# Building the state-space output matrices on one engine, and working more expert blocks ahead of the gates

## The chip, the cores and the metric

The kernel runs on one core of a Trainium2 chip. The metric is the device time of one execution in microseconds (us), the median of several. The engines are TensorE (PE; its weight loads are shown as PEld), VectorE (DVE), ScalarE (ACT), GpSimd (POOL) and SyncE (SP), which only issues DMAs here.

## What is computed

Two layers over 512 latent tokens and 256 context tokens of width 1024. Layer 0 mixes tokens with a bidirectional diagonal state-space model, layer 1 with latent attention. After each mixer comes an expert channel mixer: each token chooses 128 of 16384 experts, and

```
out = sum over k of gelu(h . U[idx_k]) * gate_k * V[idx_k]
```

In layer 0 the state-space part is, for 64 groups of 16 channels and 64 complex states each, in both directions,

```
h[t] = A h[t-1] + B u[t]          (A diagonal, complex)
y[t] = Re(C h[t]), both directions summed, plus d * u[t]
o    = (gelu(y) * sigmoid(gelu(y) @ w_glu)) @ w_o
```

The context is scanned first and hands its last state to the latent tokens. A modulation (scale, shift and gate per channel, from `ada_w`) is computed from the conditioning vectors.

## The kernel before

**Writing order.** Each stage is a Python generator that yields a planned cost after each piece of work. `merge` advances the stream whose clock is lowest, which sets the order in which instructions are written down; the streams after `side=` are advanced the same way but need not end. The framework then orders each engine's instructions by that order and by when it believes operands are ready, and waits for a free buffer where a pool has none. `t4` tiles (4 KB per partition, 20 buffers), `t2` tiles (2 KB, 8 buffers) and `row` tiles (5 buffers) are shared by all stages.

**State-space layer.** The 768 tokens are 96 chunks of eight. `s5_prep` brings the inputs to chunk states `X`; `s5_scan` runs 47 steps of four small VectorE instructions each (L645 twice, L656, L657), each planned at `TS` = 0.95; `s5_fill` completes the states in between for one block of four group pairs (VectorE L495, L498, then ScalarE L669 to L671, which reorder real and imaginary parts). `s5_mout` builds the output matrices: 8 blocks times 2 directions, each piece two halves of three elementwise instructions (L626, L627, L628) into a `t4` tile `Mout` and a `t2` scratch `tqm`, planned at `TM`. Before, a piece runs on GpSimd unless its number `b * 2 + d` is in `MV`, where it runs on VectorE. `s5_readout` goes over eight blocks: TensorE multiplies the inputs with a Toeplitz kernel `Tt` (L694) and the states with `Mout` (L697), ScalarE applies GELU (L700), TensorE turns the result (L714) and VectorE copies it out of PSUM to `yc` and `yl` (L716, L717). `products` asks `mout` for matrices as it needs them. The scan is merged with `mout` and with the modulation stream `rest` (96 tiles `ada_wt` in all, TensorE L197) beside it, the readout with `rest`. Then follow the GLU (`zp`, L762) and the output projection.

**Expert mixer.** Four tiles of 128 tokens in layer 0 and three in layer 1 are computed densely: every expert's activation, times a gate matrix that is mostly zero. The other tiles (two, then one) gather rows of U and V by index (L1287 on GpSimd's queue), with one VectorE instruction for each row (L1294, L1299); the gather's rows are spread over the other work by planned cost. For the dense tiles:

- A *U block* (128 experts) is split into a high and a low fp32r part (ScalarE L305, then VectorE or GpSimd L306), multiplied in 24 matmuls `s_ps` (L1149), and passed through GELU (L1152).
- *Gates*: one-hot matrices on VectorE (L1080, L1088), widened on ScalarE (L1085), multiplied into `g_ps` (L1102), copied to `stage` (L1104) and stored to DRAM as `gm`.
- *V blocks*: the gated activations times V in `acc` (L1219, the last half in L1240).

`ahead` works the first `A0` (layer 0) or `A1` (layer 1) U blocks before or while the gates are made, with the low part on GpSimd, and stores the activations to DRAM (`ged`). `dense` reloads them; for the other blocks the low part is VectorE's. A reloaded block is charged `-XM` = -2.0 in the plan, a fresh one 5.2 (times three quarters in layer 1). `peer` merges the gates with all but the last `TL` = 3 of the blocks worked ahead and has the gather beside them, then merges `dense` with the gather:

```
merge(self.gates, most(), side=(self.gathering,))
merge(self.dense(l), self.gathering)
```

Dense works in groups of eight blocks, first V on half the columns, then on the other half; where the next group's blocks are all worked ahead, their gating is mixed into the second half.

Of the kernel before, what the change touches and what calls it, by code (L numbers as in the profile page):

```python
# [15 lines left out]
ALU = mybir.AluOpType  # L16
# [5 lines left out]
KD = 8  # L22
# [3 lines left out]
NCH = 96  # L26
CH_CTX = 32
# [14 lines left out]
NPOOL = 0  # L42
FA = 1.0
R0, R1 = 2.25, 3.0
A0, A1 = 40, 48
GA = 5
TL, PW, XM = 3, 2, 2.0
FG0, FG1 = 50.0, 5.0
KB = 2
TP, TM, TS, TA = 4.7, 6.5, 0.95, 1.6  # L50
LA, LD = 2, 5
LT = 3
PA, FP = 20, 3.0
# [1 line left out]
AT = 2  # L55
E0, E1, E2 = 0, 11, 5
YB, YC = 1, 17
NF, MV = 2, (11, 13, 15)


def dap(t, off, ap):
    return bass.AP(tensor=t.tensor, offset=t.offset + off, ap=ap)
# [45 lines left out]
class Net:  # L108
# [240 lines left out]
    def s5_params(self):  # L349
# [106 lines left out]
        for r, op in ((0, ALU.subtract), (1, ALU.add)):  # L456
            w3 = self.t4([128, 64, 16], "w3")
            E = (V, GP)[r]
            E.tensor_tensor(out=fB[r], in0=Bt[r], in1=frb, op=ALU.mult)
            E.tensor_tensor(out=w3, in0=Bt[1 - r], in1=fib, op=ALU.mult)  # L460
            E.tensor_tensor(out=fB[r], in0=fB[r], in1=w3, op=op)
        self.ada0 = ada

    def s5_input(self):
# [10 lines left out]
        for s in (1, 0):  # L475
            c0, n = ((CH_CTX, 64), (0, CH_CTX))[s]
            for x in range(2):
                us = self.u[x][:, :, c0:c0 + n]
                m = [ms[s][:, i, x * 4:(x + 1) * 4, :].rearrange("p k r -> p (k r)").unsqueeze(2).to_broadcast([128, 32, n])
                     for i in range(2)]  # L480
                E = (V, GP)[x]
                E.tensor_tensor(out=us, in0=us, in1=m[1], op=ALU.mult)
                E.tensor_tensor(out=us, in0=us, in1=m[0], op=ALU.add)
# [116 lines left out]
    def s5_mout(self):  # L600


        GP, V = self.nc.gpsimd, self.nc.vector
        NB, pq = 4, self.pq
        sh = [128, 4, 8, 16]
        self.Mout = {}
        C = {}
        for d in range(2):
            for i in range(2):
                C[d, i] = self.t4([128, 32, 2, 16], f"cc{i}")  # L610
                self.load(C[d, i], self.a["s5_cc"][:, i, d * 32:(d + 1) * 32])
            self.nc.scalar.mul(C[d, 0][64:128], C[d, 0][64:128], -1.0)
        for b in range(8):
            for d in range(2):
                M = self.Mout[d, b] = self.t4([128, NB, 2, 128], "Mout")
                for h in range(2):
                    g0 = b * NB + h * 2
                    mo = M[:, h * 2:h * 2 + 2].rearrange("p g x (j c) -> p (g x) j c", j=8)
                    if d:
                        mo = mo[:, :, ::-1, :]  # L620
                    p = [pq[r][:, :, d * 32 + g0:d * 32 + g0 + 2, :].rearrange("p k g x -> p (g x) k").unsqueeze(3)
                         .to_broadcast(sh) for r in range(2)]
                    c = [C[d, i][:, g0:g0 + 2].rearrange("p g x c -> p (g x) c").unsqueeze(2).to_broadcast(sh) for i in range(2)]
                    tq = self.t2(sh, "tqm")
                    E = V if b * 2 + d in MV else GP
                    E.tensor_tensor(out=mo, in0=p[0], in1=c[0], op=ALU.mult)  # L626
                    E.tensor_tensor(out=tq, in0=p[1], in1=c[1], op=ALU.mult)  # L627
                    E.tensor_tensor(out=mo, in0=mo, in1=tq, op=ALU.subtract)  # L628
                yield TM

    def s5_scan(self):
# [41 lines left out]
    def s5_readout(self, mout):  # L673

        nc = self.nc
        V, S, PE = nc.vector, nc.scalar, nc.tensor
        X = self.X
        self.yT = {1: [], 0: []}

        def kernels(fb):  # L680
            Tt = self.t4([128, 8, 128], "Tt")
            for j in range(8):
                self.load(Tt[j * 16:(j + 1) * 16], dap(self.kext, fb * 8 * 3840 + (7 - j) * 16, [[240, 16], [3840, 8], [1, 128]]))
            return Tt

        def products(fb, Tt):
            while (1, fb) not in self.Mout:
                next(mout)
            yp = [self.ps([NCH, 4, 128], f"yp{g2}") for g2 in range(2)]
            for gi in range(8):  # L690
                g = fb * 8 + gi
                gp, g2 = g // 2, g % 2
                o = yp[g2][:, gi // 2, :]
                PE.matmul(out=o, lhsT=self.u[g // 32][:, g % 32, :], rhs=Tt[:, gi, :], start=True, stop=False)  # L694
                for d in range(2):
                    dg = d * 32 + gp
                    PE.matmul(out=o, lhsT=X[:, :, g2, dg], rhs=self.Mout[d, fb][:, gp % 4, g2, :], start=False, stop=(d == 1))  # L697
            Y = self.t4([NCH, 8, 8, 16], "Y")
            for g2 in range(2):
                S.activation(out=Y[:, :, g2::2, :].rearrange("p j g c -> p g j c"),  # L700
                             in_=yp[g2].rearrange("p g (j c) -> p g j c", j=8), func=AF.Gelu)
            return Y

        def turn(fb, Y):
            if fb % 4 == 0:
                self.yT[1].append(self.t4([128, 4, T_CTX], "yc"))
            if fb % 2 == 0:
                self.yT[0].append(self.t4([128, 2, T_LAT], "yl"))
            yc = self.yT[1][-1][:, fb % 4, :].rearrange("p (c j) -> p j c", j=8)
            yl = self.yT[0][-1][:, fb % 2, :].rearrange("p (c j) -> p j c", j=8)  # L710
            for j4 in range(2):
                tp = self.ps([128, 4, NCH], "ytp")
                for j in range(4):
                    PE.transpose(out=tp[:, j, :], in_=Y[:, j4 * 4 + j].rearrange("p g c -> p (g c)"),  # L714
                                 identity=self.ident[0:NCH, 0:NCH])
                V.tensor_copy(out=yc[:, j4 * 4:j4 * 4 + 4, :], in_=tp[:, :, 0:CH_CTX])  # L716
                V.tensor_copy(out=yl[:, j4 * 4:j4 * 4 + 4, :], in_=tp[:, :, CH_CTX:NCH])  # L717

        Y = None
        Tt = kernels(0)  # L720
        yield 0.0
        for fb in range(NF):
            self.s5_fill(fb)
        for fb in range(KD):
            if fb + NF < KD:
                self.s5_fill(fb + NF)
            nxt = kernels(fb + 1) if fb + 1 < KD else None
            last, Y = Y, products(fb, Tt)
            Tt = nxt
            if last is not None:  # L730
                turn(fb - 1, last)
            yield 8.0
        turn(KD - 1, Y)

    def load_w(self, src, name, n=D):
# [899 lines left out]
```

## Time and profile before

| | |
|---|---|
| median of 3 runs | 4044.7 us (4038.66 to 4044.82) |
| profiled execution, its own time | 4041.79 us |
| span of its profile | 4040.0 us |
| mean granted TensorE clock | 0.955 |
| PE busy | 3658.0 us (91%) |
| DVE busy | 3263.9 us (81%) |
| POOL busy | 1650.8 us (41%) |
| ACT busy | 1494.6 us (37%) |

Busy is the time in which an engine had an instruction in work, waiting inside it included. Line numbers are those of the kernel before. A group names the output tile, then the inputs.

### The profile page before, as it was taken

Reading aid. Unit: us, or ns where it says so; the run is one execution under the profiler, and the core shown is the slowest. Engines: PE = TensorE matmul, PEld = TensorE weight load, DVE = VectorE, ACT = ScalarE, POOL = GpSimd, SP = SyncE. Lnnn points to the kernel's source line nnn. Section 1 sums busy time; section 2 is a strip of 40 time slices with the busy share of each in tenths; the row PEclk is TensorE's granted clock in tenths of the full one; section 3 lists DMA queues with packets and bytes.
Section 4 is the critical chain, followed back from the end, with each engine's and each line's share of the span. In section 5 each row is a group of like instructions: output and inputs, shape, how many; then the busy total and the mean of one; then the engine's idle time right before and its main releaser. Section 6 shows DMA issues by size and latency. Waiting matters only on the chain.

```text
span 4040.0 us, 53946 instructions
## 1 busy us (share of the span) xinstructions
PE 3658.0 (91%) x18795; PEld 3026.4 (75%) x18795; DVE 3263.9 (81%) x6315; ACT 1494.6 (37%) x2580; POOL 1650.8 (41%) x1140
## 2 busy tenths in 40 slices
PE   6759878799699999999999989988899899999998
PEld 3527867588677878778888855568798779999997
DVE  9784498999777888888888844469998678878887
ACT  1321335356432322233332233354465333433333
POOL 4743346256422455556555300055355113334341
PEclk7879989899899999999999999999899999999999
DMA  5457234269998899999999920144378888888885
GB/s 180 129 179 251 92 113 152 81 229 317 323 330 291 287 347 331 348 352 332 341 335 341 325 99 3 33 158 150 115 250 307 294 272 320 294 330 292 328 301 212
DMA packets 398449, 986.15 MB, mean 244 GB/s; under 512 B 67040, under 2 KB 147424, under 8 KB 393568
## 3 DMA queue, kind: packets, MB, share of 16 engines
q1 hardware_dynamic: 217120, 501.34, 35.6%
q0 software_dynamic: 110592, 402.70, 28.0%
q10 hardware_dynamic: 70464, 78.65, 5.8%
q8 instruction: 148, 2.42, 0.2%
q14 instruction: 125, 1.02, 0.1%
HBM read 892.28 MB, written 90.21 MB: 243 GB/s over the span
## 4 chain that ended last, share of the span: by engine, by line
PE 46%; issue 13%; POOL 8%; DVE 8%; DMA 4%; ACT 1%; ACTq 0%; POOLq 0%; SPq 0%; DVEq 0%
PE s_ps L1149 20%; PE acc L1219 17%; POOL row L1287 6%; POOL Ul L306 2%; PE g_ps L1102 1%; PE op_mla L1519 1%; DMA row<-in_peer_v,idx 1%; DMA W<-in_peer_v 1%; DMA ge<-ged 1%; DMA U<-in_peer_uT 1%; PE acc L1240 1%; PE sp_mla L1497 1%; PE tp_ps L286 1%; PE vp L1441 1%; PE kp_mla L1475 1%
## 5 line engine op out<-in xcount | busy, mean ns | idle before, releaser
L1219 PE MATMUL acc<-Ws,A 128*128 128x512 f32 x5208 | 1199.1, 391 | 63.8 <-ACT A L305 36.2
L1149 PE MATMUL s_ps<-Hs,Uh 128*128 128x512 f32 (+1 forms) x4096 | 1185.8, 371 | 5.4 <-ACT Uh L305 5.4
L1219 PEld LDWEIGHTS acc<-Ws,A 128*128 128x128 f32 x5208 | 980.1, 189 | 278.6 <-ACT A L305 37.0
L1287 POOL DMA_INDIRECT row<-in_peer_u,idx x384 | 527.8, 1374 | 803.1 <-DVE row L1294 742.0
L1149 PEld LDWEIGHTS s_ps<-Hs,Uh 128*128 128x128 f32 x4096 | 762.7, 190 | 98.7 <-ACT Uh L305 6.6
L1149 PE MATMUL s_ps<-Hs,Ul 128*128 128x512 f32 (+1 forms) x2048 | 760.5, 371 | 38.4 <-POOL Ul L306 38.4
L1287 POOL DMA_INDIRECT row<-in_peer_v,idx x384 | 485.1, 1263 | 547.2 <-DVE f L1299 491.6
L1294 DVE SCALAR_TENSOR_TENSOR row<-row,m 128x1024 f32<-128x1024 f32 x384 | 485.7, 1280 | 51.0 <-DMA row<-in_peer_u,idx 50.0
L1299 DVE SCALAR_TENSOR_TENSOR f<-row,act,f 128x1024 f32<-128x1024 f32 x381 | 487.7, 1280 | 42.2 <-DMA row<-in_peer_v,idx 41.0
L305 ACT CAST Ws<-W 128x512 fp32r<-128x512 f32 x512 | 306.0, 619 | 488.0 <-DMA W<-in_peer_v 429.8
L1149 PEld LDWEIGHTS s_ps<-Hs,Ul 128*128 128x128 f32 x2048 | 389.5, 190 | 93.2 <-POOL Ul L306 46.8
L306 DVE TENSOR_TENSOR Ws<-W,Ws 128x512 fp32r<-128x512 f32 x512 | 345.8, 685 | 104.4 <-ACT Ws L305 104.0
L305 ACT CAST Uh<-U 128x1024 fp32r<-128x1024 f32 x256 | 268.0, 1049 | 340.6 <-DMA U<-in_peer_uT 274.5
L1152 ACT ACTIVATE ge<-s_ps 128x512 f32<-128x512 f32 (+1 forms) x256 | 139.3, 544 | 510.5 <-PE s_ps L1149 476.0
L306 POOL TENSOR_TENSOR Ul<-U,Uh 128x1024 fp32r<-128x1024 f32 x88 | 224.4, 2551 | 247.1 <-ACT Uh L305 186.5
L306 POOL TENSOR_TENSOR Wos<-wo,Wos 128x512 fp32r<-128x512 f32 x60 | 88.1, 1496 | 471.8 <-PE tp_ps L286 350.3
L1102 PE MATMUL g_ps<-o,o 128*128 128x128 f32 x1792 | 222.8, 284 | 44.5 <-DVE o L1088 33.4
L305 ACT CAST A<-ge 128x512 fp32r<-128x512 f32 (+1 forms) x256 | 144.5, 565 | 300.2 <-DVE ge L1200 294.1
L1102 PEld LDWEIGHTS g_ps<-o,o 128*128 128x128 f32 x1792 | 219.5, 200 | 48.1 <-ACT o L1085 34.6
L306 DVE TENSOR_TENSOR Ul<-U,Uh 128x1024 fp32r<-128x1024 f32 x168 | 205.0, 1221 | 45.4 <-ACT Uh L305 45.0
L1200 DVE TENSOR_TENSOR ge<-ge,Gt 128x512 f32<-128x512 f32 (+1 forms) x256 | 155.4, 620 | 72.5 <-ACT ge L1152 47.3
L306 DVE TENSOR_TENSOR A<-ge,A 128x512 fp32r<-128x512 f32 (+1 forms) x256 | 158.6, 620 | 45.5 <-ACT A L305 44.6
(345 smaller groups left out, 4600.5 us busy)
## 6 DMA issues: line engine op xcount, KB each, us to landing
U<-in_peer_uT SPq DMA_DIRECT2D x256, 512.0 KB
W<-in_peer_v SPq DMA_DIRECT2D x512, 256.0 KB
gm<-stage ACTq DMA_DIRECT2D x28, 2048.0 KB
ada_wt<-in_ada_w SPq DMA_DIRECT2D x96, 512.0 KB
Gt<-gm SPq DMA_DIRECT2D x16, 2048.0 KB
Gt<-gm SPq DMA_DIRECT2D x16, 1536.0 KB
wq<-in_peer_w_q SPq DMA_DIRECT2D x40, 512.0 KB
wo<-in_s_w_o SPq DMA_DIRECT2D x48, 256.0 KB
```

What stands on the lines that cost most here:

```text
L286: nc.tensor.transpose(out=ps[:, b, :], in_=src[:, (b0 + b) * 128:(b0 + b + 1) * 128], identity=self.ident)
L305: self.nc.scalar.copy(out=hi, in_=x)
L306: lo_eng.tensor_tensor(out=lo, in0=x, in1=hi.bitcast(F32), op=ALU.subtract)
L1102: PE.matmul(out=gp[:, t, :], lhsT=o[1][:, t4 * 4 + t, :], rhs=o[0][:, t4 * 4 + t, :], start=True, stop=True)
L1149: PE.matmul(out=sp, lhsT=x[:, k, :], rhs=self.Hs[:, y, k, :], start=(n == 0), stop=(n == 3 * KD - 1))
L1152: S.activation(out=ge, in_=sp, func=AF.Gelu)
L1200: V.tensor_tensor(out=gv, in0=gv, in1=Gt[b // SB][:, :, :, b % SB, :], op=ALU.mult)
L1219: PE.matmul(out=acc[hf][d], lhsT=A[b][:, x, c], rhs=Ws[:, y], start=(j == 0 and n == 0), stop=(j == SB - 1 and n == 2))
L1240: PE.matmul(out=acc, lhsT=A[(NS - 1) * SB + j][:, x, c], rhs=last[j][:, y], start=(j == 0 and n == 0), stop=(j == SB - 1 and n == 2))
L1287: GP.indirect_dma_start(out=r, out_offset=None, in_=tab, in_offset=bass.IndirectOffsetOnAxis(ap=ik[:, k:k + 1], axis=0), element_offset=l ...
L1294: x = V.scalar_tensor_tensor(out=r, in0=r, scalar=1.0, in1=m, op0=ALU.mult, op1=ALU.mult, accum_out=act[:, k:k + 1])
L1299: x = V.scalar_tensor_tensor(out=f, in0=r, scalar=act[:, k:k + 1], in1=f, op0=ALU.mult, op1=ALU.add)
```

## The change

The output matrices are all built on VectorE, and their planned cost `TM` rises from 6.5 to 12.0. `products` asks for the matrices of one block more than it is about to use. The turned outputs are copied out of PSUM by ScalarE instead of VectorE, in another order of the same elements. `A0` and `A1` rise by eight each.

```diff
-A0, A1 = 40, 48
+A0, A1 = 48, 56
-TP, TM, TS, TA = 4.7, 6.5, 0.95, 1.6
+TP, TM, TS, TA = 4.7, 12.0, 0.95, 1.6
-NF, MV = 2, (11, 13, 15)
+NF = 2
...
-                    E = V if b * 2 + d in MV else GP
-                    E.tensor_tensor(out=mo, in0=p[0], in1=c[0], op=ALU.mult)
-                    E.tensor_tensor(out=tq, in0=p[1], in1=c[1], op=ALU.mult)
-                    E.tensor_tensor(out=mo, in0=mo, in1=tq, op=ALU.subtract)
+                    V.tensor_tensor(out=mo, in0=p[0], in1=c[0], op=ALU.mult)
+                    V.tensor_tensor(out=tq, in0=p[1], in1=c[1], op=ALU.mult)
+                    V.tensor_tensor(out=mo, in0=mo, in1=tq, op=ALU.subtract)
...
-            while (1, fb) not in self.Mout:
+            while (1, min(fb + 1, KD - 1)) not in self.Mout:
                 next(mout)
...
-                V.tensor_copy(out=yc[:, j4 * 4:j4 * 4 + 4, :], in_=tp[:, :, 0:CH_CTX])
-                V.tensor_copy(out=yl[:, j4 * 4:j4 * 4 + 4, :], in_=tp[:, :, CH_CTX:NCH])
+                for y, c in ((yc, slice(0, CH_CTX)), (yl, slice(CH_CTX, NCH))):
+                    S.copy(out=y[:, j4 * 4:j4 * 4 + 4, :].rearrange("p j c -> p c j"), in_=tp[:, :, c].rearrange("p j c -> p c j"))
```

## Rows read from the trace of the kernel before

**Rows 1.** Merged chain of waits: start us, us, engine, tile, line, count.

```profile
1847.18 43.53 PE acc L1219 x192
1890.72 44.79 PE s_ps L1149 x192
...
2968.52 3.57 PE g_ps L1102 x32
...
3623.52 33.70 PE s_ps L1149 x192
```

**Rows 2.** Timeline, two scan steps' first instructions: start us, us, engine, line, operation.

```profile
178.58 0.49 DVE L645 TENSOR_TENSOR w<-X,a 128x128 f32<-128x128 f32 x2
...
179.63 0.49 DVE L645 TENSOR_TENSOR w<-X,a 128x128 f32<-128x128 f32 x2
```

**Rows 3.** Windows, 188 to 236 us: all instructions, then line 657 (one per step).

```profile
188.00:236.00 48.00, 17.03 (x60) 2.36 (x60) 47.21 (x45) 1.05 (x1) 47.78 (x42) 0.72 0.55 206
...
188.00:236.00 48.00, 10.37 (x10) 0.72 0.55 206
```

The columns of the first row are PE, PEld, DVE, ACT and POOL busy with instruction counts, granted TensorE clock, DMA share, GB/s; of the second DVE, clock, DMA share, GB/s.

**Rows 4.** Timeline, first fill, last output matrix, last turned-output copy.

```profile
266.49 1.03 DVE L495 TENSOR_TENSOR adv<-X,a 128x384 f32<-128x384 f32 x2
...
353.97 0.68 DVE L626 TENSOR_TENSOR Mout<-pq,cc 128x512 f32<-128x512 f32 x1
...
354.57 0.68 DVE L628 TENSOR_TENSOR Mout<-Mout,tqm 128x512 f32<-128x512 f32 x1
...
374.86 0.62 DVE L717 COPY yl<-ytp 128x256 f32<-128x256 f32 x1
```

**Rows 5.** Windows, layer 0: all instructions twice, then L1149 and L1102 alone.

```profile
840.00:1078.00 238.00, 218.70 (x1422) 198.24 (x1421) 236.83 (x236) 152.60 (x229) 136.49 (x72) 0.96 0.88 297
...
1117.00:1348.00 231.00, 223.43 (x962) 183.54 (x963) 181.29 (x300) 70.84 (x120) 67.23 (x53) 0.97 0.85 304
...
840.00:1095.00 255.00, 116.84 (x480) 88.71 (x480) 0.97 0.90 304
...
840.00:1095.00 255.00, 123.83 (x997) 122.01 (x995) 0.97 0.90 304
```

The first window is the gate stage, the second five groups of V blocks with reloaded activations.

**Rows 6.** Windows, layer 1: all instructions twice, then L1149 and L1102 alone.

```profile
2960.00:3117.00 157.00, 147.59 (x1032) 145.94 (x1033) 148.59 (x125) 99.29 (x150) 94.99 (x47) 0.98 0.86 287
3146.00:3358.00 212.00, 202.23 (x865) 162.86 (x866) 163.10 (x288) 81.08 (x147) 35.84 (x30) 0.99 0.84 285
...
2960.00:3117.00 157.00, 86.50 (x434) 78.11 (x435) 0.98 0.86 287
...
2960.00:3117.00 157.00, 69.78 (x592) 69.21 (x592) 0.98 0.86 287
```

**Rows 7.** Groups by line, 0 to 700 us: busy us, mean ns, then idle before.

```profile
L628 POOL TENSOR_TENSOR Mout<-Mout,tqm 128x512 f32<-128x512 f32 x26 | 35.9, 1390 | 0.2
...
L717 DVE COPY yl<-ytp 128x256 f32<-128x256 f32 x16 | 10.0, 635 | 0.0
...
L950 ACT COPY qT<-qp 128x256 f32<-128x256 f32 x24 | 8.0, 381 | 31.1 <-PE qp L945 31.1
```

**Rows 8.** Windows, the readout, all instructions.

```profile
248.00:375.50 127.50, 111.21 (x665) 73.63 (x664) 92.79 (x194) 36.19 (x66) 46.99 (x36) 0.94 0.73 224
```

**Rows 9.** Groups by line, 840 to 1078 us; the last row gives ns min/median/max.

```profile
L1088 DVE TENSOR_TENSOR o<-e,gT 128x1024 f32<-128x1024 bf16 x58 | 85.3, 1475 | 0.0
L1294 DVE SCALAR_TENSOR_TENSOR row<-row,m 128x1024 f32<-128x1024 f32 x54 | 78.3, 1453 | 0.0
...
L306 POOL TENSOR_TENSOR Ul<-U,Uh 128x1024 fp32r<-128x1024 f32 x19 | 50.2, 2641 | 15.5 <-ACT Uh L305 11.1 <-issue 4.2
...
L1294 DVE SCALAR_TENSOR_TENSOR row<-row,m x79: 1207/1212/3414, 851.9 to 1195.1; 128x1024 f32<-128x1024 f32 x79
```

**Rows 10.** Timeline, the end of layer 0: last row product, last `acc`.

```profile
2301.80 1.28 DVE L1299 SCALAR_TENSOR_TENSOR f<-row,act,f 128x1024 f32<-128x1024 f32 x1 [1.14 <-DMA row<-in_peer_v,idx]
...
2331.96 0.40 PE L1240 MATMUL acc<-Ws,A 128*128 128x512 f32 x1
```

More of the change, by code (lines that the diff above doesn't have):

```diff
@@ L600, in s5_mout @@
     def s5_mout(self):
-        GP, V = self.nc.gpsimd, self.nc.vector
+        V = self.nc.vector
         NB, pq = 4, self.pq
```

## The prediction

> **What bounds the kernel now.** I read the merged chain of waits first, because it says which engine each long stage follows. In the dense stages it is TensorE alone, in a fixed alternation: 192 `s_ps` matmuls (eight U blocks) in 44.79 us and 192 `acc` matmuls (eight V blocks) in 43.53 us with the four tiles of layer 0; eight U blocks in 33.70 us with the three of layer 1 [rows 1]. A U block taken out of these stages is thus worth 5.6 us in layer 0 and 4.2 us in layer 1, and nothing on VectorE or GpSimd there is worth anything by itself. One `s_ps` matmul costs 0.233 us (0.1755 in layer 1), one `g_ps` matmul 3.57 / 32 = 0.112 us.
>
> Next come the stretches that the change touches. The state-space scan is VectorE's. A scan step that nothing disturbs takes 179.63 − 178.58 = 1.05 us [rows 2]. But in 188 to 236 us, where GpSimd runs 42 output-matrix instructions (busy 47.8 of 48 us), only 10 of the 47 steps were done, 4.8 us each [rows 3]. VectorE shows 47.2 us busy there, yet ten steps are 10.5 us of work: it stands blocked inside its instructions. The reader is to see that "busy" here is mostly blocking, and that GpSimd's help costs VectorE some 37 us on the path that everything else waits for. The scan began about 177.5 (one step before the first row) and ends at 266.5 us, where the first fill starts [rows 4].
>
> Last the gate stages, which take the extra U blocks. In layer 0 VectorE is busy 236.8 of 238 us and TensorE 218.7. TensorE's real load until the last U block ends at 1095 is 480 × 0.233 + 997 × 0.112 = 112 + 111 = 223 of 255 us [rows 5]. In layer 1 it is 434 × 0.1755 + 592 × 0.112 = 76 + 66 = 142 of 157 us [rows 6].
>
> **The change, part by part.**
>
> *Scan.* The 13 pieces on GpSimd (a piece is one direction of one block, six instructions) go to VectorE, where such an instruction takes 0.68 us with GpSimd quiet [rows 4]; GpSimd's subtractions take 1.39 [rows 7]. With the pace 12.0 against 47 × 0.95 = 44.65 units of scan, the merge puts four pieces into the scan (at 0, 12, 24, 36): 4 × 6 × 0.68 = 16.3 us. New scan: 47 × 1.05 + 16.3 + 2 us, an estimate, for the modulation's few additions = 68 us; now 89. Gain 21. The loads of the C tiles keep their place in SyncE's queue; until they land VectorE has its own steps to run.
>
> *Readout.* Now 266.5 to 375.5, the last turned-output copy [rows 4]: 109 us. Afterwards VectorE has three fills (8 instructions each, 1.03 us for two [rows 4]) = 12.4; five blocks with a fill and two pieces, 5 × (4.1 + 8.2) = 61.5; one block with two pieces, 8.2: 82 us. From the last product matrix (355.25) to the last copy are 20 us [rows 4], which stay. Sum 102: gain 7. The turned-output copies leave VectorE (16 of 0.635 us [rows 7] and 16 smaller ones). On ScalarE I price all 32 by its 128x256 copy out of PSUM, 0.381 us [rows 7]: 12.2 us, counted at nothing, since ScalarE is busy 36 of 127.5 us [rows 8]. If that cover were gone, 12 us would come on the path: behind a waiting copy stand ScalarE's fill copies and GELUs, and TensorE's next products wait for those.
>
> State-space sum −28. Bounds: two matrix instructions on VectorE start 0.60 apart [rows 4], not 0.68, which gives 96 × 0.08 = 8 more, −36; a readout that stays at 109 us with every copy exposed gives −21 + 12 = −9. I stay with the durations.
>
> *U blocks, layer 0.* Eight blocks leave the part that TensorE bounds: −44.8. TensorE has 255 − 223 = 32 us free before the last U block ends, so at least 44.8 − 32 = 13 us come back. Their eight low parts run on GpSimd, 2.64 us each, beside a saturated VectorE. What that costs VectorE now: its row products take 1.453 us there against a median of 1.212, its gate products 1.475 [rows 9]; (54 × 0.241 + 58 × 0.263) / 19 = 1.5 us per low part at least, 2.64 (its whole length) at most, so 12 to 21 us for eight. As the stage needs both engines, I take 13 and half of VectorE's 12: +19. The Trainium skill, page "SBUF — State Buffer", section "Who interferes with whom", says that a VectorE instruction with two SBUF inputs and a GpSimd instruction that reads SBUF shut each other out for a whole instruction, which speaks against this half of the change. By that rule alone eight low parts would take 8 × 2.64 = 21 us from VectorE; the rows show at least 1.5 of the 2.64 each, so the trace is on its side without settling the size.
>
> The 8 × 1.2 us of low parts that leave VectorE in the dense stage are worth nothing, as TensorE covers them. The extra group of V blocks without U work between them should run like the five such groups now: 231 us [rows 5], 46.2 each against 43.53, +2.7. Each block worked ahead adds a store on ScalarE's queue and a load on SyncE's, and its U load moves ahead of the gates; DMA is at 0.88 in that stage [rows 5], so I charge nothing, a loose end.
>
> *The gather of layer 0.* The merge paces it against the dense stage. Dense loses 8 × 5.2 units for U and 8 × 2.0 for the negative charge of a ready block, 57.6, of which a few come back because the U blocks now outlast the gates. Now the last row product starts at 2301.8 and the last `acc` ends near 2332, 30 us later [rows 10]. With half of the shift absorbed where VectorE has nothing left to prepare, that lead is gone, and the second context tile's layer norm falls behind the dense end: +8 us (0 to 15) before the attention layer's first projections. Layer 0: −44.8 + 19 + 2.7 + 8 = −15, bounds −32 and +11 (the stage longer by all 44.8).
>
> *U blocks, layer 1.* −33.7. Of the 15 free us [rows 6] I let 10 be used: +24. The extra group: 212 us for six [rows 6], 35.3 each against three quarters of 43.53, +2.7. The gather keeps a lead, as the U blocks outlast the gates by some 22 of the 47 units that dense loses. Sum −7, bounds −15 (all free time used, no extra group) and +3.
>
> Total −28 − 15 − 7 = −50. The profiled execution took 4041.8 us (span 4040.0), so 3992; the median of the runs is 2.9 us higher, and I say 3994. The forecast's own range is 3970 to 4018.
>
> **Rivals**, from the median.
>
> *The U blocks come back at full price (0.15).* Both gate stages grow by what the dense stages lose. For it: both engines are nearly full there; against it: the 32 free us. Layer 0 +11, layer 1 +3: 4044.7 − 28 + 14 = 4031.
>
> *The readout does not get shorter (0.14).* It follows TensorE (busy 111 of 127.5 us [rows 8], with the modulation's weights in its queue), and the copies show. 4044.7 − 9 − 22 = 4014. Against it: part of that busy time is waiting on loads, which a quicker scan starts earlier.
>
> *Slower (0.06): the 4 KB buffers run out in the readout.* There are 20. In the sixth block these live: two power tables, four C tiles, four output matrices instead of two, two kernels, two Y, five turned outputs, one advance: 20. If VectorE must wait with a matrix until TensorE frees one, blocks go one after the other: 12.3 us of VectorE and 111 / 8 = 13.9 of TensorE, 26.2 instead of 12.3 for six blocks, +83: 4044.7 + 33 = 4078. It decides once a block takes over 12.3 + 50 / 6 = 20.6 us.
>
> *Nothing (0.05): the first two rivals together*, −9 + 14: about 4048, within what can be told.
>
> **How the numbers follow.** The forecast has 0.60. Faster by over 0.2% (8 us, about what a measurement of this kernel can tell from no change): 0.60 + 0.15 + 0.14 = 0.89; within, 0.05; slower, 0.06. The range goes from just under the forecast's own good end to the full-price rival, 3968 to 4031; it leaves out the last two rivals and thin ends, under 0.2.
>
> **What would show it.** Right: scan steps 1.05 us apart with matrix instructions of 0.68 us between, the first fill near 245, the last turned copy (ScalarE's) near 347; the first `acc` of layer 0 only about 9 us earlier than now (28 − 19); 104 low parts on GpSimd, 152 on VectorE. Wrong: matrix instructions on VectorE that wait for `yp` to free a buffer, a first `acc` of layer 0 later than now, or TensorE idle after the last `acc` of layer 0 while rows still run.

## The result, and the profile after

The changed kernel takes 4080.9 us (4077.7 to 4081.6, four runs) against 4044.4: a ratio of 1.009, 95% interval 1.0077 to 1.0103. It is 36 us slower; 3994 was predicted. The profiled execution took 4081.6 (span 4079.4).

Cut at the first or last instruction of a line, the two traces give this (us; a line's "last" is the start of its last matmul):

| stretch | before | after | change | predicted |
|---|---|---|---|---|
| start to last scan step | 266.2 | 242.7 | −23.5 | −21 |
| readout: to first `zp` | 107.9 | 111.4 | +3.5 | −7 |
| layer 0: to first `acc` | 742.7 | 768.3 | +25.6 | +19 |
| layer 0 dense: first to last `acc` | 1215.2 | 1177.3 | −37.9 | −42.1 |
| layer 0 tail: to last `kvp` (key projection) | 67.1 | 104.3 | +37.2 | +8 |
| attention: to last `op_mla` | 252.6 | 251.2 | −1.4 | 0 |
| layer 1: to first `acc` | 494.5 | 550.3 | +55.8 | +24 |
| layer 1 dense: first to last `acc` | 875.1 | 850.7 | −24.4 | −31 |
| last `acc` to the end | 18.7 | 23.2 | +4.5 | 0 |
| sum | 4040.0 | 4079.4 | +39.4 | −50.1 |

Two rows carry 61 of the 90 us by which the sum was missed: the tail of layer 0 (29 us more than predicted) and the gate stage of layer 1 (32 more). The readout adds 10.

**State-space part.** Windows of the changed kernel, 188 to 236 us, all instructions and then the scan's line 656 (columns as in [rows 3], the second row VectorE alone):

```profile
188.00:236.00 48.00, 25.32 (x92) 4.83 (x92) 45.83 (x154) 1.39 (x2) 0.00 (x0) 0.80 0.74 269
...
188.00:236.00 48.00, 8.76 (x30) 0.80 0.74 269
```

GpSimd is silent, and 30 steps run where [rows 3] has 10, with a run of matrix instructions (15 us, 0.60 apart) between two of them. VectorE is as busy as before, now with its own work. The timeline of VectorE and ScalarE at the end of the scan and of the readout:

```profile
243.05 1.03 DVE L495 TENSOR_TENSOR adv<-X,a 128x384 f32<-128x384 f32 x2
...
320.60 1.28 DVE L627 TENSOR_TENSOR Mout<-Mout,tqm 128x512 f32<-128x512 f32 x2
...
352.21 0.69 DVE L207 TENSOR_TENSOR ada_r<-ada_ps,abias 128x512 f32<-128x512 f32 x1 [30.32 <-PE ada_ps L197]
...
354.56 0.40 ACT L716 COPY yl<-ytp 128x256 f32<-128x256 f32 x1
```

VectorE is through 79 us after the first fill (82 predicted), where [rows 4] has its last matrix at 354.57. Then it has nothing to do for 30 us: the last copy comes 33 us after the last matrix, where 20 were assumed.

**End of layer 0.** Timeline of TensorE and VectorE:

```profile
2295.65 4.47 PE L1239 MATMUL acc<-Ws,A 128*128 128x512 f32 x19
...
2302.77 1.68 PE L296 MATMUL mt_ps<-ident,h 128*128 128x128 f32 x8 [2.66 <-DMA h<-hd]
...
2304.24 5.64 PE L1376 MATMUL kvp<-wkv,mT 128*128 128x320 f32 x16
...
2320.75 1.28 DVE L1298 SCALAR_TENSOR_TENSOR f<-row,act,f 128x1024 f32<-128x1024 f32 x1 [0.40 <-DMA row<-in_peer_v,idx]
...
2340.54 1.97 PE L296 MATMUL mt_ps<-ident,h 128*128 128x128 f32 x8 [30.66 <-DMA h<-hd]
```

`acc` now ends at 2300, but the last gathered row is multiplied at 2320.75, 21 us behind it; in [rows 10] it was 30 us ahead. The second context tile has yet to be normalised, stored and loaded, and TensorE stands still for 30.66 us. The 32 us that dense ended earlier are gone, and 5 more.

**Gates of layer 1.** Windows of the changed kernel, first to last `g_ps` and on to the first `acc`: line 1148 (`s_ps`) alone (the columns are then PE and PEld), and all instructions of the second stretch; the last two rows are the same stretches of the kernel before, its line 1149 alone.

```profile
2853.00:3125.00 272.00, 168.58 (x842) 154.40 (x842) 0.96 0.69 226
3125.00:3206.00 81.00, 49.19 (x238) 46.10 (x238) 0.80 0.68 259
...
3125.00:3206.00 81.00, 49.69 (x239) 46.60 (x240) 17.26 (x27) 16.35 (x23) 34.34 (x21) 0.80 0.68 259
...
2843.00:3111.00 268.00, 163.38 (x816) 149.97 (x816) 0.95 0.68 223
3111.00:3146.00 35.00, 15.91 (x72) 14.96 (x72) 0.73 0.97 364
```

In the kernel before, 816 `s_ps` matmuls run between first and last `g_ps` and 72 after. So one more block (24 matmuls) fits among the gates, and the other seven come behind them, where VectorE is mostly idle (17 of 81 us busy). There they don't even run at TensorE's pace. Timelines of PE, POOL and SP (SyncE), and at the end the window of 3140 to 3160 us, all instructions:

```profile
3129.55 0.51 PE L1148 MATMUL s_ps<-Hs,Uh 128*128 128x384 f32 x2
...
3141.47 0.69 PE L1148 MATMUL s_ps<-Hs,Ul 128*128 128x384 f32 x1 [11.40 <-POOL Ul L306]
3141.95 0.84 PE L1148 MATMUL s_ps<-Hs,Uh 128*128 128x384 f32 x2
...
3158.86 1.01 PE L1148 MATMUL s_ps<-Hs,Uh 128*128 128x384 f32 x2 [11.12 <-ACT Uh L305]
...
3126.89 0.95 POOL L1286 DMA_INDIRECT row<-in_peer_u,idx  x1 [1.37 <-DVE row L1293]
...
3138.84 2.58 POOL L306 TENSOR_TENSOR Ul<-U,Uh 128x1024 fp32r<-128x1024 f32 x1
...
3045.78 60.91 SPq L166 DMA_DIRECT2D U<-in_peer_uT  x9
3146.34 0.33 SPq L166 DMA_DIRECT2D Gt<-gm  x1
3146.76 0.38 SPq L166 DMA_DIRECT2D U<-in_peer_uT  x1
3147.23 0.38 SPq L166 DMA_DIRECT2D Gt<-gm  x1
3147.72 23.46 SPq L166 DMA_DIRECT2D U<-in_peer_uT  x7
...
3140.00:3160.00 20.00, 7.28 (x24) 6.45 (x24) 4.79 (x6) 1.53 (x2) 8.08 (x6) 0.59 1.02 400
```

Two stalls, two queues. The first low part stands on GpSimd behind seven row gathers, each of which waits for VectorE to free a row buffer. And SyncE has a `Gt` load ahead of eight U loads; `Gt` reads the gate matrix, whose last store SyncE awaits until 3146. After each stall, in which TensorE had stood still, two matmuls take 0.84 us instead of 0.51 for a while; the granted clock was 0.59 in 3140 to 3160, so TensorE ran at 1.2 instead of 2.4 GHz for most of it.

### The profile page after: what moved, and what is told of

Read it like the earlier page. It is cut to its first block, busy times and chain, and to the rows that moved or that the text cites. A ratio compares the mean times of both kernels' runs of the same rounds, so it can differ in the third digit from the quotient of the medians.

```text
span 4079.4 us, 54051 instructions
## 1 busy us (share of the span) xinstructions
PE 3675.3 (90%) x18795; PEld 3030.7 (74%) x18795; DVE 3245.5 (80%) x6345; ACT 1501.3 (37%) x2612; POOL 1585.3 (39%) x1078
## 4 chain that ended last, share of the span: by engine, by line
PE 39%; issue 13%; DVE 8%; DMA 7%; POOL 6%; ACT 1%; POOLq 0%; SPq 0%; ACTq 0%; DVEq 0%
PE s_ps L1148 17%; PE acc L1218 14%; POOL row L1286 5%; DMA row<-in_peer_v,idx 2%; DMA W<-in_peer_v 1%; POOL Ul L306 1%; DMA U<-in_peer_uT 1%; DMA ge<-ged 1%; PE g_ps L1101 1%; PE op_mla L1518 1%; DVE row L1293 1%; DVE Ws L306 1%; PE kvp L1376 1%; PE acc L1239 1%; PE sp_mla L1496 1%
## 5 line engine op out<-in xcount | busy, mean ns | idle before, releaser
L1286 POOL DMA_INDIRECT row<-in_peer_u,idx x384 | 519.3, 1352 | 819.6 <-DVE row L1293 758.1
L1148 PE MATMUL s_ps<-Hs,Ul 128*128 128x512 f32 (+1 forms) x2048 | 765.1, 374 | 55.8 <-POOL Ul L306 55.8
L1293 DVE SCALAR_TENSOR_TENSOR row<-row,m 128x1024 f32<-128x1024 f32 x384 | 494.1, 1301 | 63.2 <-DMA row<-in_peer_u,idx 62.1
L306 POOL TENSOR_TENSOR Ul<-U,Uh 128x1024 fp32r<-128x1024 f32 x104 | 264.4, 2544 | 288.7 <-ACT Uh L305 227.0
L306 POOL TENSOR_TENSOR Wos<-wo,Wos 128x512 fp32r<-128x512 f32 x60 | 87.0, 1475 | 614.4 <-PE tp_ps L286 335.8
L306 DVE TENSOR_TENSOR Ul<-U,Uh 128x1024 fp32r<-128x1024 f32 x152 | 185.4, 1221 | 39.6 <-ACT Uh L305 38.8
```

Of the source, the lines that this page charges most:

```text
L306: lo_eng.tensor_tensor(out=lo, in0=x, in1=hi.bitcast(F32), op=ALU.subtract)
L1148: PE.matmul(out=sp, lhsT=x[:, k, :], rhs=self.Hs[:, y, k, :], start=(n == 0), stop=(n == 3 * KD - 1))
L1286: GP.indirect_dma_start(out=r, out_offset=None, in_=tab, in_offset=bass.IndirectOffsetOnAxis(ap=ik[:, k:k + 1], axis=0), element_offset=l ...
L1293: x = V.scalar_tensor_tensor(out=r, in0=r, scalar=1.0, in1=m, op0=ALU.mult, op1=ALU.mult, accum_out=act[:, k:k + 1])
```

## The experiments

All edits are to the changed kernel. Time is the median; the ratio is to the kernel before, run beside it.

**The parts alone.** The eight extra blocks worked ahead are taken back in both layers (`s5_only`), kept in layer 0 only (`l0_only`) or in layer 1 only (`l1_only`).

```diff
-A0, A1 = 48, 56
+A0, A1 = 40, 48    # s5_only;  48, 48: l0_only;  40, 56: l1_only
```

> The changed kernel with A0, A1 back at 40, 48: the state-space half of the change alone. If the parts add up as the landmarks of the two traces read (first zp 20 us earlier, first s_ps 18 us earlier): about 4025 us against 4044 before. Rival: the earlier start is lost again in the gather of layer 0 whatever the U blocks do, so that the end comes out within 8 us of before, 4037 to 4044.

> The changed kernel with A0, A1 = 48, 48: the eight extra U blocks of layer 0, none in layer 1. Additive reading: the attention layer starts 5 us later than before although the state-space part ends 18 us earlier, so layer 0's blocks cost 23 us: 4025 + 23 = 4048. Rival (the loss sits in layer 1 alone, and layer 0 is only shifted): 4030 or less.

> The changed kernel with A0, A1 = 40, 56: the eight extra U blocks of layer 1 alone. Additive reading: layer 1 is 34 us longer in the changed trace (first s_ps of layer 1 5.5 us later, end 39.4 later): 4025 + 34 = 4059. Rival (U blocks at full price, no more): gates +33.7, dense -33.7, so 4025 to 4030.

| | us | ratio (95%) |
|---|---|---|
| `s5_only` | 4029.2 | 0.9965 (0.9953 to 0.9978) |
| `l0_only` | 4055.0 | 1.0026 (1.0014 to 1.0039) |
| `l1_only` | 4052.2 | 1.0018 (1.0009 to 1.0028) |

The parts add up: −14, then +26 and +23 on top of it, +35 together against +36. So it is the extra U blocks that make the kernel slower, in both layers, while the state-space half is a gain. No version has the extra blocks without the state-space half, so that the blocks would cost the same there is not shown. (That half is worth 19.6 us at the first `zp` and 14 at the end; executions of `s5_only` lie between 4017 and 4038, so 5 us are within the scatter.)

**Layer 0: the planned cost of a row.**

```diff
-R0, R1 = 2.25, 3.0
+R0, R1 = 2.15, 3.0   # r0_low: with A0, A1 = 48, 48;  ctl_r0: with 40, 48
```

> l0_only (A0, A1 = 48, 48, 4055 us) with the planned cost of a gathered row in layer 0 at 2.15 instead of 2.25: about 452 rows are left when dense starts, so 45 units or some 50 us earlier. Theory, layer 0's blocks cost because the last row product (2320 us) falls behind the last acc (2300): rows end near 2275, key projections start for the second tile without a hole, about 25 us less than l0_only: 4030. Rival (the rows only push VectorE's other work out and dense ends later by the same): 4050 to 4058.

> The control for the cheaper row: s5_only (A0, A1 = 40, 48, 4029 us) with the planned cost of a row in layer 0 at 2.15. If a cheap row helps because the extra U blocks took away the gather's lead, there is nothing to win here, where the last row product already ends 30 us before the last acc: within 6 us of 4029. If it is a gain of its own that has nothing to do with the U blocks, 45 us as between l0_only and r0_low: 3984 to 3995.

`r0_low`: 4009.6 us, 0.9917 (0.9893 to 0.994), 45 below `l0_only`. `ctl_r0`: 4023.7, 0.9960 (0.9949 to 0.9971), no different from `s5_only`. So a cheaper row is worth nothing by itself and 45 us where the blocks ahead have taken the gather's lead. The timeline of `r0_low`:

```profile
2261.82 1.28 DVE L1298 SCALAR_TENSOR_TENSOR f<-row,act,f 128x1024 f32<-128x1024 f32 x1 [0.66 <-DMA row<-in_peer_v,idx]
...
2285.62 4.93 PE L1239 MATMUL acc<-Ws,A 128*128 128x512 f32 x21
2290.38 1.03 PE L296 MATMUL mt_ps<-ident,h 128*128 128x128 f32 x8
2291.53 4.58 PE L1376 MATMUL kvp<-wkv,mT 128*128 128x320 f32 x16
2295.94 1.04 PE L296 MATMUL mt_ps<-ident,h 128*128 128x128 f32 x8
```

Rows end 28 us ahead of `acc`, and the hole is gone. By stretches as in the first table (before, `l0_only`, `r0_low`): to first `acc` 742.7, 767.7, 770.9; dense 1215.2, 1180.2, 1165.5; tail 67.1, 103.2, 67.6. The late rows cost 36 us of tail and some 15 of dense, more than the 25 expected. Of the 15 us of dense, 8 are TensorE's waits for split V blocks (`Ws`, 20.9 us in `l0_only` and 12.5 in `r0_low`); the rest was not traced.

**Layer 1: SyncE's queue.** The first two `Gt` loads are kept in written order, behind the U loads.

```diff
-            self.load(Gt[sb], self.gm[sb])
+            x = nc.sync.dma_start(out=Gt[sb], in_=self.gm[sb])
+            if sb < 2:
+                self.tc.keep_in_program_order(x)
```

> The changed kernel with the first two Gt loads of each layer kept behind the U loads on SyncE's queue. Theory, the U loads stand behind a Gt load that waits for the last store of the gate matrix: in layer 1 the stall of 11 us near 3148 and the low clock after it go, about 20 us less, layer 0 up to 8 less: 4055 to 4062. Rival, the last blocks are slow by their own TensorE and DMA time: 4077 to 4085.

4062.9 us, 1.0044 (1.0027 to 1.0061): 18 less than the changed kernel. Timelines of PE and SP:

```profile
3137.41 0.69 PE L1148 MATMUL s_ps<-Hs,Ul 128*128 128x384 f32 x1 [11.01 <-POOL Ul L306]
...
3146.51 1.01 PE L1148 MATMUL s_ps<-Hs,Uh 128*128 128x384 f32 x2 [2.45 <-ACT Uh L305]
...
3041.01 114.42 SPq L166 DMA_DIRECT2D U<-in_peer_uT  x17
...
3184.14 0.42 SPq L1183 DMA_DIRECT2D Gt<-gm  x1
```

The stall on the U load shrank from 11.12 to 2.45 us; the one behind GpSimd's gathers stayed. Layer 1's first `acc` comes 534 us after the last `op_mla`, not 550; layer 0's is where it was (1122.1 against 1122.4): its last U block ends 8 us earlier (1110.1 against 1118.1), but TensorE then waits 12.0 us instead of 4.3 for the first gated activations, so the gated activations are next on the path there.

**Layer 1: blocks among the gates.** The plan charges a U block less, so that more of them are written before the gates end (`spread_l1`); then rows are made cheaper too (`rows_l1`).

```diff
-A0, A1 = 48, 56
+A0, A1 = 40, 56
-            return 5.2 * NT / 4
+            return (5.2 if l == 0 else 4.0) * NT / 4
...
-R0, R1 = 2.25, 3.0
+R0, R1 = 2.25, 2.8    # rows_l1 only
```

> l1_only (A0, A1 = 40, 56, 4052 us) with a U block planned at 3.0 instead of 3.9 in layer 1, so that more of them are written among the gates and fewer behind them. If the gate stage has free TensorE time that the extra blocks can use, first acc of layer 1 some 25 to 30 us earlier against the stage's start, end near 4024. If the gates get longer by what the tail loses: 4045 to 4055, but without the stall on the U load still some 10 less, 4042. If the order does not matter: 4052.

> spread_l1 (4041.5 us; last row product at 4014, 10 us behind the last acc at 4004, and 40 us from there to the end instead of 19) with a row of layer 1 planned at 2.8 instead of 3.0. Theory, the spread blocks are worth their place and the gather's tail hides it: rows end some 30 us before the last acc, 19 us of tail, 4018 to 4024. Rival, dense gets longer by what the rows take from VectorE: 4036 to 4042.

`spread_l1`: 4041.5 us, 0.9997 (0.9986 to 1.0007), 11 below `l1_only`. `rows_l1`: 4037.0, 0.9989 (0.9979 to 0.9999); the 18 to 24 us expected did not come. Layer 1 by stretches:

| | to first `acc` | dense | to the end | sum |
|---|---|---|---|---|
| before | 494.5 | 875.1 | 18.7 | 1388.3 |
| `l1_only` | 545.8 | 847.2 | 22.8 | 1415.8 |
| `spread_l1` | 514.5 | 848.9 | 40.1 | 1403.5 |
| `rows_l1` | 515.2 | 864.5 | 19.1 | 1398.8 |

Spread out (three blocks before the first `g_ps`, five among them), the blocks lengthen the gate stage by 20 us, not 51: some of the free TensorE time can be used. The windows of `spread_l1` from first to last `g_ps`, line 1148 alone, then all:

```profile
2836.00:3122.00 286.00, 181.77 (x936) 168.74 (x936) 0.96 0.67 217
...
2836.00:3122.00 286.00, 268.92 (x1753) 263.41 (x1754) 266.91 (x582) 162.65 (x238) 140.54 (x64) 0.96 0.67 217
```

936 `s_ps` matmuls, 94 more, in 14 us more than the changed kernel took for 842. But the rows then end behind dense (last one 4014.18, last `acc` 4003.6, 40 us to the end), and when they are written earlier, dense gets 16 us longer. The waits of PE around the dense stage, first of `rows_l1`, then of `spread_l1` (us in total, times, longest):

```profile
PE acc L1218 <- DVE Ws L306: 20.7, 22, 2.8
PE acc L1218 <- ACT A L305: 17.7, 1, 17.7
PE acc L1218 <- ACT Ws L305: 2.8, 4, 1.5
...
PE acc L1218 <- DVE Ws L306: 12.4, 14, 1.7
PE acc L1218 <- ACT A L305: 10.4, 1, 10.4
PE acc L1218 <- ACT Ws L305: 2.0, 5, 0.7
```

The wait for `A` ends at the first `acc` and so belongs to the gate stage. Those for the split V blocks `Ws`, most of them for VectorE, are 23.5 against 14.4 us: 9 of the 16. For the rest TensorE is busy 6 us longer with the same number of matmuls (841 against 835 us). Layer 1's eight blocks cost 10 us in the better of these versions.

**Both together.** The changed kernel with rows at 2.15 and 2.8 (`rows_both`), and with layer 1's blocks spread as well (`all_paced`).

> The changed kernel (4081 us) with rows planned at 2.15 and 2.8 and nothing else. Additive: -45 as in layer 0 between l0_only and r0_low, and about -4 in layer 1, where 23 us of tail stand against 19: 4030 to 4036. What is left against s5_only is the stall of layer 1's U loads.

> The changed kernel with rows planned at 2.15 and 2.8 and layer 1's U blocks planned at 3.0. Additive: r0_low 4009.6 and layer 1's blocks worth 5 to 8 us once spread and not late: 3999 to 4006, faster than before by 1%. If layer 1's blocks only cost: above 4012.

`rows_both`: 4038.6, 0.9995 (0.9985 to 1.0006), 42 less than the changed kernel (38 by the ratios) and 3 above the expected band. `all_paced`: 4017.5, 0.9935 (0.9915 to 0.9955): a gain, but not the 4002 expected, and no better than `r0_low`, which leaves layer 1 alone. It lies above 4012, where layer 1's blocks only cost.

**The readout.** `ada_early` moves modulation work from the readout into the scan; `s5_plain` puts the turned copies back on VectorE and undoes the look-ahead of `products`; `ada_late` writes all modulation work that is left behind the readout. Each is `s5_only` with:

```diff
-TP, TM, TS, TA = 4.7, 12.0, 0.95, 1.6      # ada_early
+TP, TM, TS, TA = 4.7, 12.0, 0.95, 1.2
-PA, FP = 20, 3.0
+PA, FP = 20, 4.0
...
-            merge(readout, rest)               # ada_late
+            merge(readout); drain(rest)
...
-            while (1, min(fb + 1, KD - 1)) not in self.Mout:   # s5_plain, and the copies
+            while (1, fb) not in self.Mout:
```

> s5_only (A0, A1 = 40, 48, 4029 us) with the modulation planned at 1.2 instead of 1.6 for each weight tile, its pace in the stage before the scan kept by a factor of 4 instead of 3: about 9 of its weight tiles move from the readout into the scan. Theory, the readout of the changed kernel is bound by TensorE (103 of 114 us busy, 34 of it modulation): scan as long as before, last turned copy 7 to 9 us earlier, about 4021. Rival, the readout follows the chain fill, product, GELU, turn: last turned copy within 2 us, 4029.

> s5_only with the turned copies back on VectorE and the look-ahead of products undone: what is left is the output matrices on VectorE and TM = 12. Theory (TensorE bounds the readout, VectorE is idle from 320 us on): no change within 3 us of s5_only, 4026 to 4032, last turned copy near 355. Rival, the moved copies carry part of the gain: 16 x 0.62 + 16 smaller copies back on VectorE, 10 us or more longer, 4039 or more.

> s5_only with the modulation that is left after the scan written behind the readout instead of beside it, so that TensorE has only the state-space products in the readout (its 38 modulation tiles there, 34 us of TensorE, follow it). The readout of s5_only takes 111 us from the last scan step to the first zp; VectorE's own part ends 34 us before that. If TensorE bounds it: the last turned copy 20 us or more earlier than 355, 335 or less. If the chain fill, product, GELU, turn bounds it whatever TensorE does beside: 350 to 355. The end is later or the same either way, as the modulation follows.

`ada_early`: 4028.6, 0.9959 (0.9947 to 0.9971); last scan step 245.4, first `zp` 357.3: 112 us, as in `s5_only` (243.0, 354.5). My theory failed this test: 28 modulation matmuls fewer, and no shorter. `s5_plain`: 4032.2, 0.9975 (0.9965 to 0.9986), first `zp` 358.6: the moved copies and the look-ahead are worth about 4 us here by the traces (the intervals of the two overlap). `ada_late`: 4052.3, 1.0028 (1.0015 to 1.0042), later as a whole since the modulation follows; but its last turned copy comes at

```profile
325.32 0.44 ACT L716 COPY yl<-ytp 128x256 f32<-128x256 f32 x1
```

84 us after the last scan step, 30 before that of `s5_only`. So without the modulation beside it the readout can follow VectorE's 79 us, and with it it takes 111. The windows from 243 us to the last copy of `ada_late`:

```profile
243.00:326.00 83.00, 71.14 (x468) 65.33 (x468) 73.07 (x135) 41.48 (x98) 0.00 (x0) 0.92 0.33 87
```

and of `s5_only`:

```profile
243.00:355.00 112.00, 101.54 (x613) 70.32 (x614) 76.98 (x146) 41.63 (x97) 0.00 (x0) 0.95 0.69 206
```

TensorE is busy 30 us longer in the second, as much as the readout is longer. Why 6.5 us less of it (`ada_early`) bought nothing is not settled: there TensorE was busy 98 of 116 us, and VectorE waited in its own queue for a modulation transpose (6.1 us) and for ScalarE's fill copies (7.7), so that its last matrix instruction started at 336.3 instead of 321.6.

**A last try.** `r0_low` with the `Gt` loads of `gt_behind`.

> r0_low (A0, A1 = 48, 48, row planned at 2.15; 4009.6 us) with the first two Gt loads behind the U loads. One U load of layer 0 stands behind a Gt load there. If the queue costs as in layer 1, in proportion: first acc of layer 0 some 5 to 8 us earlier, 4002 to 4005. If the Gt load itself is next on the path in layer 0: no change, 4006 to 4013.

4004.0 us, 0.9902 (0.9874 to 0.9929); the intervals of the two overlap. It could not tell what it was meant to: SyncE's rows of `r0_low` show both `Gt` loads (1101.31) behind all its U loads already, and first `acc` is the same (1124.1, 1124.7). These two are the fastest versions, both faster than the kernel before and the changed one.

## Why the prediction was wrong

Three terms carry 71 of the 90 us by which the sum was missed: the tail of the readout (10), the gather of layer 0 (29) and the gate stage of layer 1 (32).

*Scan (−21): right.* −23.5, by the mechanism named: scan steps 1.05 us apart, matrix instructions of 0.68 us between. They came in one run of 15 us, where 16.3 were predicted.

*Readout (−7): failed at "from the last product matrix to the last copy are 20 us, which stay".* VectorE's own 82 us came out as 79, but 20 was the tail of a readout in which TensorE kept up with VectorE. Now TensorE is behind when VectorE ends, and the tail is 33. This was the rival with 0.14 in its mechanism (it follows TensorE, with the modulation's weights in its queue). `ada_late` shows that the modulation holds the readout back; that each us of it counts is not shown (`ada_early`). The rival's other half, copies that show, is wrong: with them on VectorE the readout is 4 us longer.

*U blocks, layer 0 (gates +19, dense −42).* Both numbers are about right, +25.6 and −37.9, but the first is partly luck. Counted from the first `zp`, the last U block ends 43 us later than before (764.0 against 721.0), nearly the full 44.8: seven of the eight blocks are written among the gates and lengthen them by only 15 us, but behind the gates TensorE waits 16 us for U blocks and their low parts (1.6 before), at a granted clock of 0.81 (1073 to 1118 us; 1.00 in 1076 to 1095 before). What gave 17 us back is that a wait got shorter which the sum did not have. After the last U block TensorE stood until the first gated activations were there, for 21.68 us before (first row) and 4.33 now:

```profile
1116.79 1.95 PE L1219 MATMUL acc<-Ws,A 128*128 128x512 f32 x3 [21.68 <-ACT A L305]
...
1108.16 1.22 PE L1148 MATMUL s_ps<-Hs,Uh 128*128 128x512 f32 x2 [6.19 <-ACT Uh L305]
...
1122.43 1.95 PE L1218 MATMUL acc<-Ws,A 128*128 128x512 f32 x3 [4.33 <-ACT A L305]
```

With the gather on time (`r0_low`) the two rows are +28 and −50: −22 in all, close to the −23 predicted for them. Low parts beside VectorE did cost it time: in 840 to 1078 us there are 22 instead of 19, and the groups by line of the changed kernel show

```profile
L1087 DVE TENSOR_TENSOR o<-e,gT 128x1024 f32<-128x1024 bf16 x56 | 85.1, 1523 | 0.0
L1293 DVE SCALAR_TENSOR_TENSOR row<-row,m 128x1024 f32<-128x1024 f32 x55 | 84.0, 1531 | 3.5 <-DMA row<-in_peer_u,idx 3.5
```

against 1475 and 1453 ns in [rows 9]: 56 × 0.048 + 55 × 0.078 = 7.0 us for three more, 2.3 each, between the bounds of 1.5 and 2.64. The same window of `l0_only`, also with 22 low parts, has 1530 (x55) and 1488 ns (x56), 1.7 each, so two traces of the same stage do not settle the size. The Trainium skill, page "SBUF — State Buffer", section "Who interferes with whom", calls this contention an exclusive lock. Held for a whole low part, that would be the upper bound; both traces lie below it.

*The gather of layer 0 (+8, bounds 0 to 15): a term that failed.* It is +37, and some 50 with what the late rows do to dense. The prediction saw that the 30 us of lead in [rows 10] would go and then assumed that half of a shift of 57.6 units was absorbed, and that what was late was one layer norm. Most of it came (30 ahead to 21 behind, 51 us), and behind the last row stand a multiplication by `m`, a layer norm, a store, a load and the key projections, in series on TensorE's path. `r0_low` and its control show it. The sign that was named, TensorE idle after the last `acc` while rows still run, is what the trace has. So is another: the first `acc` of layer 0 comes 5.6 us later than before, not 9 earlier.

*U blocks, layer 1 (+24 and −31): the gate stage failed.* It is +55.8. The free 15 us were there, but the merge of gates and blocks goes by planned units, and at 3.9 a block the extra ones were not written among the gates. Behind them they cost their full price, 7 × 4.2 = 29 us, plus two stalls of 11 us and the slow clock after each; the wait for the first gated activations gave 11 back (14.56 us before, 3.39 now). `spread_l1` has +20 where +24 was predicted, and `gt_behind` takes 16 off the stage. What was missing was to ask where in the order of writing the extra blocks land, and what stands ahead of them on SyncE and GpSimd. In dense the −31 holds only while rows are late (−24 to −28); with rows in time it is −10. Even in the better placing that was tried the blocks cost 10 us here: with the sum −7 the sign was wrong, too.

*The rivals.* "Back at full price" (4031) was nearest in kind for layer 1, but no rival had a cost above the full price, and the slower one, buffers that run out in the readout, did not happen: no matrix instruction waits for `yp` in 243 to 357 us. (The sum of the first two rivals together is 4050, not 4048.)

## What to carry to other kernels

When streams are merged by planned cost, moving work out of one shifts every other stream that is paced against it: before you count the gain, see which stream ends last afterwards, and what follows its last piece in series. Here work added to a stage was hidden where it was written among the other work, and cost its full price and more behind it; look up where the order puts it, and which loads and gathers stand ahead of it on the issuing queues. A number that comes out right can hide two errors: compare its parts, too. A gain that vanishes can be got back by one number of the plan: here 2.25 to 2.15 turned +26 us of layer 0 into a gain.

## What the runs showed of the hardware

The two stalls of TensorE in layer 1 of the changed kernel cost more than their length. After 11.40 us without matmuls, pairs of `s_ps` took 0.84 us instead of 0.51 from 3141.95 to about 3146; after the next, of 11.12 us, they were slow again from 3158.86 to about 3166. By the pairs that is some 2 us on top of each stall, an estimate. And executions of one kernel scatter by 10 to 20 us here (`s5_only` 4017 to 4038), so differences of 5 us between two versions were left open.
